# First adaLN vectors by feature with the weights stationary, products taken k-tile by k-tile, rotary angles computed after the first norm, opening reordered

## The chip, the cores and the metric

The kernel runs on one core of a Trainium2 chip. The metric is the device time of one execution in microseconds (us); the figure for the kernel before is the median of 3 runs.

## The reference, cut to what matters

Two layers of a decoder trunk: x is 512 tokens by 1024 features in float32. Each layer forms six vectors of 1024 from the conditioning vector c (adaLN), normalises x, scales and shifts it by two of them, and multiplies by a large weight; q and k are rotated by angles that come from the positions.

```python
c_act = jax.nn.silu(c)
ada = jnp.einsum('bd,de->be', c_act, w_ada[l]) + b_ada[l]
sh_m, sc_m, g_m, sh_f, sc_f, g_f = jnp.split(ada, N_ADA, axis=-1)
h = rmsnorm(x, norm_mix_g[l]) * (1.0 + sc_m) + sh_m
proj = jnp.einsum('bsd,de->bse', h, w_in[l])
ang = positions.astype(jnp.float32)[..., None] * inv_freq
cos, sin = jnp.cos(ang), jnp.sin(ang)
q, k = apply_rope(q, cos, sin), apply_rope(k, cos, sin)   # t1*cos - t2*sin, t2*cos + t1*sin
```

Behind this follow differential attention, two convolution branches, a gated merge and a squared-ReLU MLP, for both layers, and a last rmsnorm. The change touches only the first adaLN vectors, the first norm's scaling, the angles and the order of the opening.

## The kernel before, in words

Activations are kept feature by token: xT[k] holds features 128k to 128k+127 of all 512 tokens, one tile per k-tile, 8 in all. Products run on TensorE in three passes, because each factor is split into a high part that TensorE's fast float32 form holds and a low part: high x high, low x high, high x low (line 145). So a weight chunk needs a cast on ScalarE (the high part, line 394, in the opening line 1270) and a subtraction on VectorE (the low part, line 402, in the opening line 1276), and a product of a 1024-deep k runs 8 x 3 matmuls of 512 columns.

**The opening** is everything up to the first four products (q and k of the first head pair). Its order is written out by hand in the table START (line 38): each word is a unit of work, a letter and a number, and the units are issued from left to right; every engine then works through its own share strictly in that order. SyncE issues the loads: positions (line 1102), x in 8 pieces (line 1110), then four times a quarter of the scale and shift columns of w_ada (8 pieces of 256 KB, line 1118) and of the first two w_in weights (line 1128). The units that matter here:

- y: the sum of squares of a piece of x (ScalarE, line 1225); x and v: four transposes on TensorE (line 1214) and a copy to xT by ScalarE (1217) or VectorE (1219); n and b: the reciprocal root and its broadcast rb.
- e and d: a part of a quarter's scale (e) and shift (d) on VectorE, the last ON_DVE k-tiles of the sum over d (lines 1183 and 1186); r and s: the rest on TensorE as rows, with the activated c broadcast over 128 stationary columns and 256 columns of w_ada moving (line 1193), and a last product that adds VectorE's part (1196); c: ScalarE copies the rows out (1299); t: four transposes turn the rows into columns (1203); q: bias added and gains formed (lines 268 and 272).
- m: two k-tiles of the norm's result are scaled, shifted and split (VectorE 484, ScalarE 487, VectorE 491).
- h and l: high and low part of a quarter of a weight; l14 and l15 also issue the next two weight loads (line 367), which reuse the two staging buffers and so wait for the last reads of those. h16 and l16 are the two parts of the first weight behind the opening.
- p: a quarter (two k-tiles) of one of the four first products; a0 to a7: the angles (VectorE 1148 to 1163, then sine and cosine on ScalarE, 1165 and 1166).

**Behind the opening** the order comes from tasks that are due after so many matmuls. Each of the four products goes through rope: ScalarE copies it out of PSUM (line 712), four loads on SyncE's queue swap its halves (714), VectorE multiplies by cos (717) and sin (719) and adds (720), the result is split (723 to 734) and moved once more by SyncE's queue (738, 739). The first scores of attention (lines 789 and 790) need that. Between the opening and these scores TensorE works on the value products, with one tiny product for the lambdas among them (line 251). SyncE's queue also carries the third weight load (line 367), behind the first eight half-swaps.

Of the kernel before, what the change touches and what calls it, by code (L numbers as in the profile page):

```python
# [10 lines left out]
F32 = mybir.dt.float32  # L11
F32R = mybir.dt.float32r
I32 = mybir.dt.int32
AF = mybir.ActivationFunctionType
ALU = mybir.AluOpType
AX = mybir.AxisListType

P = 128
D = 1024
S = 512  # L20
# [12 lines left out]
WDELAY = 1  # L33
LAM = 2

ON_DVE = ((2, 3), (1, 5), (8, 3), (3, 7))
START = (
# [4 lines left out]
)  # L42
QSTEP, COMB, AWAIT, PWAIT, PERIOD = 2, 2, 3, 4, 9
CPACE, ADA0, ADA1, APACE = 0.71, 2.36, 2.19, 1.62
# [23 lines left out]
SH_M, SC_M, G_M, SH_F, SC_F, G_F = range(6)  # L68
# [3 lines left out]
def kernel(  # L72
# [7 lines left out]
    nc = tc.nc  # L80
    V, A, T, G = nc.vector, nc.scalar, nc.tensor, nc.gpsimd
# [13 lines left out]
    def nm(s):  # L95
        cnt[0] += 1
        return f"{s}{cnt[0]}"
# [3 lines left out]
    def slot(tag, dt=F32, shape=None):  # L101
        return slots.tile(shape or [P, S], dt, tag=tag, name=nm(tag), bufs=SLOTS[tag])

    def ftile(dt=F32, shape=None):
        return slot("f", dt, shape)
# [7 lines left out]
    def ps_t():  # L113
        return psum.tile([P, S], F32, tag="t", name=nm("t"), bufs=3)
# [36 lines left out]
    def pacer(p):  # L151
# [9 lines left out]
    ident = const.tile([P, P], F32, name="ident")  # L161
# [5 lines left out]
    ones1 = const.tile([P, 1], F32, name="ones1")  # L167
# [6 lines left out]
        out=mask[:, 384:512], in_=mask[:, 384:512], pattern=[[-1, 128]],  # L174
# [82 lines left out]
    ada = [const.tile([P, 48], F32, name=f"ada{l}") for l in range(L)]  # L257
    gsc = [const.tile([P, 16], F32, name=f"gsc{l}") for l in range(L)]
    cact = const.tile([P, 8], F32, name="cact")
    ada_known = [set() for _ in range(L)]  # L260

    def ada_done(l, q, n, sm):

        v = q // 8
        dst = ada[l][:, q : q + n]
        ada_known[l].update(range(q, q + n))
        assert (l, 1 if v == SC_F else 0) in written and (l, 0) in written
        V.tensor_tensor(dst, sm, prm[l][:, C_BADA + q : C_BADA + q + n], op=ALU.add)
        if v in (SC_M, SC_F):
            f = (0 if v == SC_M else 8) + q % 8  # L270
            g0 = (C_NMIX if v == SC_M else C_NMLP) + q % 8
            V.scalar_tensor_tensor(out=gsc[l][:, f : f + n], in0=dst, scalar=1.0,
                                   in1=prm[l][:, g0 : g0 + n], op0=ALU.add, op1=ALU.mult)
        if v == G_M:
            V.tensor_scalar(out=dst, in0=dst, scalar1=0.5, scalar2=None, op0=ALU.mult)
# [175 lines left out]
    def bcast(col, n):  # L451

        pt = ps_t()
        for b in range(n):
            T.transpose(pt[:, b * P : (b + 1) * P], col[:, b : b + 1].to_broadcast([P, P]), ident)  # L455
        return pt
# [14 lines left out]


    xT = [xpool.tile([P, S], F32, name=f"xT{k}") for k in range(KD)]

    def modulate(l, f, rb, hh, ks, t0=0, t1=S):

        sv = (SH_M if f == 0 else SH_F) * 8
        assert all(q + k in ada_known[l] for k in ks for q in (sv, sv + 8))
        n = t1 - t0
        u = {}  # L480
        for k in list(ks) + [None]:
            if k is not None:
                u[k] = ftile()
                V.scalar_tensor_tensor(
                    out=u[k][:, :n], in0=xT[k][:, t0:t1], scalar=gsc[l][:, f * 8 + k : f * 8 + k + 1],
                    in1=rb[:, :n], op0=ALU.mult, op1=ALU.mult)
                A.activation(hh[k][0][:, t0:t1], u[k][:, :n], AF.Identity,
                             bias=ada[l][:, sv + k : sv + k + 1])
            if len(u) > (1 if k is not None else 0):
                j = min(u)  # L490
                V.scalar_tensor_tensor(
                    out=hh[j][1][:, t0:t1], in0=u.pop(j)[:, :n], scalar=ada[l][:, sv + j : sv + j + 1],
                    in1=hh[j][0][:, t0:t1].bitcast(F32), op0=ALU.add, op1=ALU.subtract)

    def new_h():
        return [(slot("h", F32R), slot("h", F32R)) for _ in range(KD)]
# [602 lines left out]
    rc = const.tile([P, 2], F32, name="rc")  # L1099
    A.dma_start(rc, rope_c)  # L1100
    posi = slot("at", I32)
    nc.sync.dma_start(posi, positions.to_broadcast([P, S]))
    prm_task = params(0)
    next(prm_task)
    x2 = x.rearrange("b s d -> (b s) d")
    xin = [None] * 8
    for hh in range(2):
        for i in range(NTB):
            t = xin[2 * i + hh] = slot("cv")
# [3 lines left out]
    def fetch(v, qt):  # L1113

        res = []
        for j in range(4):
            r = slot(next(stage), F32, [P, 2, 256])
            nc.sync.dma_start(r, w_ada[0, 256 * j : 256 * j + 256, v * D + qt * 256 : v * D + qt * 256 + 256]
                              .rearrange("(k p) e -> p k e", p=P))
            res.append(r)  # L1120
        return res

    raws += [wraw.tile([P, 8, 256], F32, tag="raw", name=nm("raw")) for _ in range(2)]
    quarters = []
    for qt in range(4):
        quarters.append((fetch(SC_M, qt), fetch(SH_M, qt)))
        for raw, (src, c0, _) in zip(raws, specs):
            nc.sync.dma_start(raw[:, 2 * qt : 2 * qt + 2, :],
                              src[256 * qt : 256 * qt + 256, c0 : c0 + 256].rearrange("(k p) e -> p k e", p=P))

    pt = ps_t()
    T.transpose(pt[:, :8], crow, ident[:8, :8])
# [35 lines left out]
    h = new_h()  # L1168
    parts = [adap.tile([P, 512], F32, tag="araw", name=nm("part")) for _ in range(2)]

    def part(qt, v):
        return parts[qt % 2][:, v * 256 : v * 256 + 256]

    def partial(qt, vs):

        for k in range(8):
            for v in vs:
                k0 = 8 - ON_DVE[qt][v]
                if k < k0:
                    continue  # L1180
                r = quarters[qt][v][k // 2][:, k % 2, :]
                if k == k0:
                    V.tensor_scalar(out=part(qt, v), in0=r, scalar1=cact[:, k : k + 1],
                                    scalar2=None, op0=ALU.mult)
                else:
                    V.scalar_tensor_tensor(out=part(qt, v), in0=r, scalar=cact[:, k : k + 1],
                                           in1=part(qt, v), op0=ALU.mult, op1=ALU.add)

    def rows_of(qt, v, pt):

        n = 8 - ON_DVE[qt][v]
        for k in range(n):
            T.matmul(pt[:, v * 256 : v * 256 + 256], cact[:, k : k + 1].to_broadcast([P, P]),  # L1193
                     quarters[qt][v][k // 2][:, k % 2, :], start=k == 0, stop=k == 7)
        if n < 8:
            T.matmul(pt[:, v * 256 : v * 256 + 256], ones1.to_broadcast([P, P]), part(qt, v),
                     start=n == 0, stop=True)

    def turn(row):

        pt = ps_t()
        for a in range(4):
            T.transpose(pt[:, a * P : a * P + P], row[:, a * P : a * P + P], ident)
        return pt

    def quarter_done(qt, pt):
        pv = pt.rearrange("p (a b) -> p a b", a=4)
        ada_done(0, SC_M * 8 + 2 * qt, 2, pv[:, 0:2, 0])
        ada_done(0, SH_M * 8 + 2 * qt, 2, pv[:, 2:4, 0])

    def x_turned(k, eng):
        pt = ps_t()
# [23 lines left out]
        V.tensor_scalar(out=ms, in0=ms, scalar1=1.0 / D, scalar2=None, op0=ALU.mult)  # L1236
        box["y0"] = rstd(ms, 4)

    w1, qk, q_rows, q_cols, w_tasks = [], [], {}, {}, []
    first = {}  # L1240
    box = {}
    ang_task, lam_task = angles(), lambdas()
# [47 lines left out]
            spawn(rope(first[i], qk, i))  # L1290
            run_due()

    def rows_scale(qt):
        q_rows[qt] = ps_t()
        rows_of(qt, 0, q_rows[qt])

    def rows_copy(qt):
        row = ftile()
        A.copy(row, q_rows[qt])
        q_rows[qt] = row  # L1300

    units = dict(
        x=lambda k: x_turned(k, A),
        v=lambda k: x_turned(k, V),
        y=square, n=lambda _: rms(), w=warm,
        i=lambda _: next(prm_task),
        z=lambda _: next(lam_task),
        a=lambda _: next(ang_task, None),
        b=lambda _: box.update(rb=bcast(box["y0"], 4)),
        e=lambda qt: partial(qt, (0,)),  # L1310
        d=lambda qt: partial(qt, (1,)),
        f=lambda qt: partial(qt, (0, 1)),
        r=rows_scale,
        s=lambda qt: rows_of(qt, 1, q_rows[qt]),
        c=rows_copy,
        t=lambda qt: q_cols.update({qt: turn(q_rows[qt])}),
        q=lambda qt: quarter_done(qt, q_cols[qt]),
        m=lambda qt: modulate(0, 0, box["rb"], h, (2 * qt, 2 * qt + 1)),
        h=high, l=low,
        p=lambda n: first_product(n // 4, n % 4),  # L1320
    )
# [7 lines left out]
    for l in range(L):  # L1329
        merged = mixer(l, h, qk, NF if l else 4)  # L1330
        f = []
        h = closing(l, G_M, merged, l, 1,
                    lambda pp, i: relu2(pp, f, ff_tags(0, i)))
        if l + 1 < L:
            pace["ada"] = APACE
        f = mlp(l, h, f, NF)
        if l + 1 < L:
            qk = []
            h = closing(l, G_F, f, l + 1, 0, lambda pp, i: rope(pp, qk, i))
# [38 lines left out]
```

## Time and profile before

| | |
|---|---|
| median of 3 runs | 1906.89 us (1906.71 to 1907.18) |
| profiled execution, whole time | 1904.28 us |
| its span, first to last instruction | 1902.5 us |
| TensorE matmuls busy | 1874.3 us (99% of the span) |
| VectorE, ScalarE busy | 1256.0 us (66%), 785.8 us (41%) |
| mean granted TensorE clock | 0.997 |

The profile shows one execution. An engine's row in a timeline gives its start and duration, how many instructions of one kind it merges, and in brackets the idle time before it with the instruction that ended the wait. The chain of waits follows the work that ended last back through whatever released each step. PE is TensorE, PEld its weight loads, DVE VectorE, ACT ScalarE, SP SyncE; a q behind a name means its queue of issued instructions. A float32 product that is not in the fast form shows as two records of MATMUL.

### The profile page before, as it was taken

The numbers are of one execution on the slowest core, as the hardware profiler recorded it, in microseconds if no ns is written. First come the engines' busy times: TensorE is split into PE (matmuls) and PEld (weight loads), VectorE is DVE, ScalarE is ACT, GpSimd is POOL, SyncE is SP. The second block draws the span as 40 slices with busy tenths as digits, with TensorE's granted clock in tenths as the row PEclk, the third lists the DMA queues.
The fourth block names the chain that finished last, engine by engine and source line by source line (L and its number), as shares of the span: only waits on it lengthen the run. The fifth ranks groups of instructions, "written<-read, shape, count | busy, mean of one in ns | idle before, by whom it ended". The sixth has DMA issues, their size and how long they took to land.

```text
span 1902.5 us, 24972 instructions
## 1 busy us (share of the span) xinstructions
PE 1874.3 (99%) x9565; PEld 1599.9 (84%) x9565; DVE 1256.0 (66%) x2139; ACT 785.8 (41%) x1420; POOL 63.4 (3%) x109
## 2 busy tenths in 40 slices
PE   8999999999999999999999999999999999999998
PEld 6788888888889888888898888888888898888888
DVE  7788789996676556565677777898654563333336
ACT  4466652223333524333445666322243353424253
POOL 1011010000000000000000000000000000000000
PEclk9999999999999999999999999999999999999999
DMA  8644323444554455555535442232233422223221
GB/s 272 181 130 126 101 67 98 151 138 145 166 178 135 139 178 195 177 185 182 171 97 142 123 122 73 89 104 96 67 100 100 133 89 89 89 93 106 89 89 67
DMA packets 211527, 241.20 MB, mean 127 GB/s; under 512 B 10408, under 2 KB 178480, under 8 KB 211408
## 3 DMA queue, kind: packets, MB, share of 16 engines
q1 hardware_dynamic: 210480, 239.38, 40.6%
q8 instruction: 75, 1.23, 0.3%
q0 software_dynamic: 768, 0.23, 0.1%
q14 instruction: 44, 0.36, 0.1%
q10 hardware_dynamic: 160, 0.01, 0.0%
HBM read 216.50 MB, written 2.10 MB: 115 GB/s over the span
## 4 chain that ended last, share of the span: by engine, by line
PE 93%; DMA 3%; DVE 2%; issue 1%; SPq 1%; ACT 1%; POOL 0%; POOLq 0%; DVEq 0%; ACTq 0%
PE mm L145 83%; PE s L145 3%; DMA f<-f 2%; PE t L817 1%; PE s L789 1%; PE s L790 1%; PE t L806 1%; SPq L714 1%; PE t L1193 1%; PE t L455 0%; PE t L303 0%; PE t L825 0%; POOL st L438 0%; DVE f L719 0%; PE t L1214 0%
## 5 line engine op out<-in xcount | busy, mean ns | idle before, releaser
L145 PE MATMUL mm<-h,wh 128*128 128x512 f32 x2720 | 851.3, 392 | 0.0
L145 PEld LDWEIGHTS mm<-h,wh 128*128 128x128 f32 x2720 | 509.6, 188 | 103.3
L145 PE MATMUL mm<-h,wl 128*128 128x512 f32 x1360 | 533.6, 392 | 0.0
L394 ACT CAST wh<-raw 128x1024 fp32r<-128x1024 f32 (+1 forms) x308 | 308.9, 1005 | 407.2 <-PE mm L145 358.2
L402 DVE TENSOR_TENSOR wl<-raw,wh 128x1024 fp32r<-128x1024 f32 (+1 forms) x308 | 358.2, 1166 | 69.6 <-ACT wh L394 65.9
L145 PE MATMUL mm<-qk,wh 128*128 128x512 f32 (+1 forms) x1024 | 300.2, 376 | 0.0
L145 PEld LDWEIGHTS mm<-h,wl 128*128 128x128 f32 x1360 | 256.2, 188 | 51.9
L145 PEld LDWEIGHTS mm<-qk,wh 128*128 128x128 f32 x1024 | 188.2, 188 | 35.1
L145 PE MATMUL mm<-qk,wl 128*128 128x512 f32 (+1 forms) x512 | 192.6, 376 | 0.0
L912 DVE SCALAR_TENSOR_TENSOR cv<-v,caw,cv 128x511 f32<-128x511 f32 (+14 forms) x240 | 176.0, 733 | 4.2
L499 DVE SCALAR_TENSOR_TENSOR xT<-mm,ada,xT 128x512 f32<-128x512 f32 (+1 forms) x81 | 56.0, 691 | 151.2 <-PE mm L145 151.0
L281 DVE SCALAR_TENSOR_TENSOR araw<-araw,cact,araw 128x512 f32<-128x512 f32 x140 | 104.6, 747 | 25.2 <-DMA araw<-in_w_ada_dram 24.7
L145 PEld LDWEIGHTS mm<-qk,wl 128*128 128x128 f32 x512 | 96.3, 188 | 17.2
L1059 ACT ACTIVATE f<-mm 128x512 f32<-128x512 f32 x60 | 35.9, 598 | 160.6 <-PE mm L145 160.6
L145 PE MATMUL mm<-o,wh 128*128 128x512 f32 (+1 forms) x320 | 95.5, 381 | 0.0
L145 PE MATMUL mm<-v,wh 128*128 128x512 f32 (+1 forms) x320 | 94.9, 379 | 0.0
L145 PE MATMUL mm<-wh,h 128*128 128x256 f32 x448 | 84.1, 284 | 0.0
L761 ACT ACTIVATE cv<-cv,st 128x128 f32<-128x128 f32 (+3 forms) x128 | 71.0, 558 | 25.6 <-DVE st L754 25.2
L1033 DVE SCALAR_TENSOR_TENSOR f<-f,mm 128x512 f32<-128x512 f32 x38 | 26.1, 687 | 83.6 <-PE mm L145 83.6
L469 DVE TENSOR_TENSOR qk<-f,qk 128x512 fp32r<-128x512 f32 x38 | 26.3, 691 | 77.4 <-ACT qk L466 77.2
L438 POOL TENSOR_TENSOR st<-st,nhalf 128x4 f32<-128x4 f32 (+2 forms) x29 | 31.2, 1076 | 1368.0 <-DVE st L460 1013.4
L145 PEld LDWEIGHTS mm<-wh,h 128*128 128x128 f32 x448 | 70.8, 191 | 0.4
(259 smaller groups left out, 2282.9 us busy)
## 6 DMA issues: line engine op xcount, KB each, us to landing
raw<-in_w_in_dram SPq DMA_DIRECT2D x66, 1024.0 KB, 5.2
raw<-in_w_ff_dram SPq DMA_DIRECT2D x64, 1024.0 KB, 5.4
araw<-in_w_ada_dram SPq DMA_DIRECT2D x160, 256.0 KB, 3.0
f<-f SPq DMA_DIRECT2D x128, 64.0 KB, 2.0
qk<-qk SPq DMA_DIRECT2D x64, 128.0 KB, 2.6
raw<-in_w_c_out_dram SPq DMA_DIRECT2D x8, 1024.0 KB, 5.0
raw<-in_w_out_dram SPq DMA_DIRECT2D x8, 1024.0 KB, 5.0
qk<-in_w_ada_dram SPq DMA_DIRECT2D x16, 256.0 KB, 6.0
```

Source lines behind the costliest of these rows:

```text
L145: T.matmul(ps, lhsT, rhs, start=start, stop=stop)
L281: V.scalar_tensor_tensor(out=part, in0=r, scalar=cact[:, k : k + 1], in1=part, op0=ALU.mult, op1=ALU.add)
L394: A.copy(h_, r_)
L402: V.tensor_tensor(l_, r_, h_.bitcast(F32), op=ALU.subtract)
L438: G.tensor_tensor(y, v[:, :n], nhalf[:, :n], op=ALU.pow)
L469: V.tensor_tensor(lo, src, hi.bitcast(F32), op=ALU.subtract)
L499: V.scalar_tensor_tensor(out=xT[e][:, t0:t1], in0=pp[:, t0:t1], scalar=g[:, e : e + 1], in1=xT[e][:, t0:t1], op0=ALU.mult, op1=ALU.add)
L714: nc.sync.dma_start(sw[32 * q : 32 * q + 32, :], t[32 * (q ^ 1) : 32 * (q ^ 1) + 32, :])
L761: A.activation(p[cc][:, :n], p[cc][:, :n], AF.Exp, bias=nb[:, cc : cc + 1], scale=-1.0, accum_out=l0[:, i : i + 1] if cc == 0 else s1)
L912: V.scalar_tensor_tensor(out=ac[:, s:], in0=glu[j][:, : S - s], scalar=wk, in1=ac[:, s:], op0=ALU.mult, op1=ALU.add)
L1033: V.scalar_tensor_tensor(out=t, in0=t, scalar=1.0, in1=pp, op0=ALU.add, op1=ALU.mult)
L1059: A.activation(r, pp, AF.Relu)
```

## The change

The scale and shift columns are no longer made as rows and turned. In the new units r and s the 128 x 128 block of w_ada is the stationary operand and the one column of c moves, so the result stands by feature at once; units c and t (row copy, four transposes) are gone. ON_DVE is a little larger (34 k-tiles on VectorE, before 32). The unit m is split into u (scale, and the high part) and g (the low part), one k-tile at a time, and e and d are issued by single k-tiles. The load of positions is issued behind all loads of the opening, and the angles a0 to a7 stand behind the first norm, nearly at the end of START. Eleven products of the identity with itself (w11) stand ahead of the first transposes. Five of the x tiles are copied by VectorE, before four.

```diff
-ON_DVE = ((2, 3), (1, 5), (8, 3), (3, 7))
+ON_DVE = ((5, 4), (1, 4), (5, 4), (7, 4))
-    "i0 a0 y1 x1 a1 a2 y0 i1 y2 a3 v0 a4 x2 v7 y3 a5 v5 e0 y4 y7 y6 y5 v3 n h2 d0 r0 h0 l2 z "
...
+    "l8 p5 d37 l14 h10 l15 g4 g5 r31 l10 i2 s30 l11 s31 p8 q3 l9 h12 u6 u7 l13 l12 g6 h16 g7 a0 a1 "
+    "a2 a3 p11 p10 p9 l16 a4 a5 a6 a7 p12 p13 p14 p15"
...
-    nc.sync.dma_start(posi, positions.to_broadcast([P, S]))
...
+    nc.sync.dma_start(posi, positions.to_broadcast([P, S]))
...
-            T.matmul(pt[:, v * 256 : v * 256 + 256], cact[:, k : k + 1].to_broadcast([P, P]),
-                     quarters[qt][v][k // 2][:, k % 2, :], start=k == 0, stop=k == 7)
-        if n < 8:
-            T.matmul(pt[:, v * 256 : v * 256 + 256], ones1.to_broadcast([P, P]), part(qt, v),
-                     start=n == 0, stop=True)
...
+            T.matmul(dst, quarters[qt][v][k // 2][:, k % 2, b * P : b * P + P], cact[:, k : k + 1],
+                     start=k == 0, stop=k == 7)
+        if n < 8:
+            T.matmul(dst, part(qt, v)[:, b * P : b * P + P], ones1, start=n == 0, stop=True)
...
+    def scaled(k):
+        u_[k] = ftile()
+        V.scalar_tensor_tensor(out=u_[k], in0=xT[k], scalar=gsc[0][:, k : k + 1], in1=box["rb"],
+                               op0=ALU.mult, op1=ALU.mult)
+        A.activation(h[k][0], u_[k], AF.Identity, bias=ada[0][:, SH_M * 8 + k : SH_M * 8 + k + 1])
+
+    def scaled_low(k):
+        V.scalar_tensor_tensor(out=h[k][1], in0=u_.pop(k), scalar=ada[0][:, SH_M * 8 + k : SH_M * 8 + k + 1],
+                               in1=h[k][0].bitcast(F32), op0=ALU.add, op1=ALU.subtract)
```

How the instructions move. The end of the opening on VectorE before: h are the low parts of the normed input, wl the last low part of the opening's weights, f_624 the copy of the first product, cv_632 the high part of the first weight behind the opening.

```order
L484 SCALAR_TENSOR_TENSOR f_607<-xT_111,gsc_101,t_367 128x512
L491 SCALAR_TENSOR_TENSOR h_237<-f_604,ada_99,h_236 128x512
L491 SCALAR_TENSOR_TENSOR h_239<-f_607,ada_99,h_238 128x512
L1276 TENSOR_TENSOR wl_246<-raw_143,wh_245 128x256
L717 TENSOR_TENSOR f_640<-f_624,cos_t 128x512
L402 TENSOR_TENSOR cv_653<-raw_584,cv_632 128x512
```

The same place on VectorE now, from the last h on; at_120 are the positions, at_222 and at_223 the angles, rc the frequencies, cv_638 and cv_639 the low part of the first weight behind the opening.

```order
L1275 SCALAR_TENSOR_TENSOR h_239<-f_603,ada_99,h_238 128x512
L1130 CAST at_222<-at_120 128x512
L1131 TENSOR_SCALAR at_222<-at_222,rc 128x512
L1133 TENSOR_SCALAR at_223<-at_222 128x512
L1135 TENSOR_SCALAR at_223<-at_223 128x512
L1138 SCALAR_TENSOR_TENSOR at_222<-at_223,at_222 128x512 x2
L404 TENSOR_TENSOR cv_638<-raw_559,cv_609 128x512
L404 TENSOR_TENSOR cv_639<-raw_559,cv_610 128x512
L1138 SCALAR_TENSOR_TENSOR at_222<-at_223,at_222 128x512
L1140 TENSOR_SCALAR at_223<-at_222 128x512
L1142 SCALAR_TENSOR_TENSOR at_223<-at_222,at_223 128x512
L1145 TENSOR_SCALAR at_222<-at_222 128x512
```

All eleven angle instructions (one more L1145 follows) now stand between the last h and the first multiplication by cos, and the two low parts of the next weight stand among them.

ScalarE before, from the last two h to the first rope copies; h_236 and h_238 are high parts of the normed input, f_624 and f_646 copies of the first two products, cv_632, cv_633 and wh_638 high parts of weights. (Sine and cosine stand 18 instructions earlier, behind the cast of wh_247.)

```order
L487 ACTIVATE h_236<-f_604,ada_99 128x512
L487 ACTIVATE h_238<-f_607,ada_99 128x512
L712 COPY f_624<-mm_444 128x512
L394 CAST cv_632<-raw_584 128x512
L394 CAST cv_633<-raw_584 128x512
L394 CAST wh_638<-raw_584 128x1024
L712 COPY f_646<-s_456 128x512
```

ScalarE now, the same place; f_655 is the copy of the first product.

```order
L1272 ACTIVATE h_236<-f_600,ada_99 128x512
L1272 ACTIVATE h_238<-f_603,ada_99 128x512
L396 CAST cv_609<-raw_559 128x512
L396 CAST cv_610<-raw_559 128x512
L1147 ACT_TABLE_LOAD
L1147 ACTIVATE sin_t<-at_222,rc 128x512
L1148 ACTIVATE cos_t<-at_223 128x512
L694 COPY f_655<-mm_451 128x512
L396 CAST wh_664<-raw_559 128x1024
L694 COPY f_672<-s_476 128x512
```

Ahead of the copy of the first product now stand the two casts of the next weight, a table load, the sine and the cosine. From the rows that follow these on, all five engines issue the same instructions in the same order as before.

More of the change, by code (lines that the diff above doesn't have):

```diff
@@ L473 @@
     xT = [xpool.tile([P, S], F32, name=f"xT{k}") for k in range(KD)]
[L475 to L493, printed above, removed]
     def new_h():
@@ L1172, in part @@
         return parts[qt % 2][:, v * 256 : v * 256 + 256]
[L1174 to L1187, printed above, removed]
@@ L1189, in rows_of, with partial @@
-    def rows_of(qt, v, pt):
+    def partial(qt, k, v):
+        k0 = 8 - ON_DVE[qt][v]
+        if k < k0:
+            return
+        r = quarters[qt][v][k // 2][:, k % 2, :]
+        if k == k0:
+            V.tensor_scalar(out=part(qt, v), in0=r, scalar1=cact[:, k : k + 1],
+                            scalar2=None, op0=ALU.mult)
+        else:
+            V.scalar_tensor_tensor(out=part(qt, v), in0=r, scalar=cact[:, k : k + 1],
+                                   in1=part(qt, v), op0=ALU.mult, op1=ALU.add)
@@ L1191, in rows_of, with columns @@
+    def columns(qt, v, b):
+        if v == 0 and b == 0:
+            q_cols[qt] = ps_t()
         n = 8 - ON_DVE[qt][v]
+        dst = q_cols[qt][:, 2 * v + b : 2 * v + b + 1]
         for k in range(n):
-            T.matmul(pt[:, v * 256 : v * 256 + 256], cact[:, k : k + 1].to_broadcast([P, P]),
-                     quarters[qt][v][k // 2][:, k % 2, :], start=k == 0, stop=k == 7)
+            T.matmul(dst, quarters[qt][v][k // 2][:, k % 2, b * P : b * P + P], cact[:, k : k + 1],
+                     start=k == 0, stop=k == 7)
@@ L1195, in rows_of @@
         if n < 8:
-            T.matmul(pt[:, v * 256 : v * 256 + 256], ones1.to_broadcast([P, P]), part(qt, v),
-                     start=n == 0, stop=True)
[L1199 to L1204, printed above, removed]
+            T.matmul(dst, part(qt, v)[:, b * P : b * P + P], ones1, start=n == 0, stop=True)
     def quarter_done(qt, pt):
-        pv = pt.rearrange("p (a b) -> p a b", a=4)
-        ada_done(0, SC_M * 8 + 2 * qt, 2, pv[:, 0:2, 0])
-        ada_done(0, SH_M * 8 + 2 * qt, 2, pv[:, 2:4, 0])
+        ada_done(0, SC_M * 8 + 2 * qt, 2, pt[:, 0:2])
@@ L1211, in x_turned @@
+        ada_done(0, SH_M * 8 + 2 * qt, 2, pt[:, 2:4])
     def x_turned(k, eng):
@@ L1237, in rms @@
         box["y0"] = rstd(ms, 4)
-    w1, qk, q_rows, q_cols, w_tasks = [], [], {}, {}, []
+    w1, qk, u_, q_cols, w_tasks = [], [], {}, {}, []
     first = {}
@@ L1291, in first_product @@
             run_due()
[L1293 to L1300, printed above, removed]
+    def scaled(k):
[6 more added lines that the diff above has]
+                               in1=h[k][0].bitcast(F32), op0=ALU.add, op1=ALU.subtract)
     units = dict(
@@ L1309 @@
         b=lambda _: box.update(rb=bcast(box["y0"], 4)),
[L1310 to L1316, printed above, removed]
+        e=lambda n: partial(n // 10, n % 10, 0),
+        d=lambda n: partial(n // 10, n % 10, 1),
+        r=lambda n: columns(n // 10, 0, n % 10),
+        s=lambda n: columns(n // 10, 1, n % 10),
         q=lambda qt: quarter_done(qt, q_cols[qt]),
-        m=lambda qt: modulate(0, 0, box["rb"], h, (2 * qt, 2 * qt + 1)),
+        u=scaled, g=scaled_low,
         h=high, l=low,
```

7 rows, old and new, of the table START are left out of this document.

## The prediction

> **What bounds the kernel now.** The first line of the page gives the span; the profiled execution took 1904.28 us as a whole, 1.8 more, and the median of the runs is 1906.89, 2.6 above that. I work out a difference on the profiled execution and add it to the median.
>
> ```profile
> span 1902.5 us, 24972 instructions
> ```
>
> TensorE is busy nearly throughout, and the order of instructions shows no difference on any engine behind the opening. So the change is worth what it does to the moment at which the unchanged rest starts. I read next what TensorE waits for in the first 140 us (waiter, releaser: us in total, times, longest), and the stretches around these waits (stretch, PE, PEld, DVE, ACT, POOL busy, clock, DMA).
>
> ```profile
> PE t L207 <- DMA f<-in_norm_mix_g_dram: 6.1, 1, 6.1
> PE s L789 <- DMA qk<-f: 3.2, 1, 3.2
> PE s L789 <- DVE st L754: 1.8, 2, 1.1
> ```
> ```profile
> 10.90:51.83 40.93, 40.79 (x195) 34.57 (x195) 36.79 (x88) 21.32 (x48) 6.84 (x12) 1.00 0.85 269
> 75.00:80.00 5.00, 3.77 (x11) 3.11 (x12) 2.12 (x7) 0.99 (x4) 0.00 (x0) 0.66 0.79 200
> ```
>
> In the opening TensorE never stops (40.79 of 40.93 us) and VectorE is close behind (36.79). The first wait for something else is 3.2 us, in front of the first attention scores (L789), and the clock drops behind it. What sets the time of these scores is read from the chain of waits (start, us, what) and from SyncE's queue.
>
> ```profile
> 8.96 5.40 PE t L1214 x24
> ...
> 31.98 0.44 PE t L1203 x4
> ...
> 53.87 0.59 ACT f L712
> ...
> 59.87 5.71 DMA raw<-in_w_in_dram
> ...
> 65.61 1.06 ACT wh L394
> ...
> 76.65 0.45 PE s L789
> ...
> 77.31 4.97 PE mm L145 x16
> ...
> 82.76 3.65 PE mm L145 x16
> ```
> ```profile
> 48.27 4.35 SPq L367 DMA_DIRECT2D raw<-in_w_in_dram  x2
> 54.48 5.29 SPq L714 DMA_DIRECT2D f<-f  x8
> ```
>
> ScalarE copies the first product at 53.87. Then SyncE's queue issues the eight half-swaps of the first two products without a pause (54.48, for 5.29 us), and only then the third weight load (its transfer from 59.87). ScalarE, which works in order, needs that load for a cast at 65.61, ahead of the copy of the fourth product, and the rest of rope follows to the scores at 76.65. Every step waits for the one before: from the copy at 53.87 to the scores is a fixed distance, and TensorE, out of other work 3.2 us earlier, waits for its end.
>
> **The change part by part.** *Columns on TensorE.* A record of the old form (256 columns moving) takes 0.216 us, from the first to the next group below (17.61 to 19.77 for 10); the new form (128 x 128 stationary, one column) stands in the trace as line 447.
>
> ```profile
> 17.61 2.32 PE L1193 MATMUL t<-qk,cact 128*128 128x256 f32 x10
> 19.77 0.59 PE L1196 MATMUL t<-part,ones 128*128 128x256 f32 x2
> ...
> 454.83 0.95 PE L447 MATMUL t<-inv,f 128*128 128x1 f32 x8
> 455.63 0.64 PE L303 MATMUL t<-ident,araw 128*128 128x128 f32 x4
> ```
> ```profile
> L447 PEld LDWEIGHTS t<-inv,f 128*128 128x128 f32 x16 | 2.1, 191 | 0.2
> ```
>
> Before: 32 products and 8 closings, two records each, 80 x 0.216 = 17.3 us, and 16 turns at 0.11 (0.44 for 4), 1.8: 19.1 us. Now 30 products in two halves and 16 closings, 76, two records each: 152 x 0.10 = 15.2 us (455.63 - 454.83 over 8). The other end, weight loads of 191 ns one after the other, would give 29.0. I take 0.10, the spacing seen, so TensorE has 3.9 us less. The 11 warming products stand in the first wait of 6.1 us and cost nothing there; if they bring the clock up, the first 24 transposes cost 0.11 instead of 0.225 each (5.40 for 24), 2.8 us less.
>
> *VectorE.* If TensorE does less, VectorE is the next late engine of the opening.
>
> ```profile
> 10.90 0.69 DVE L1219 COPY xT<-t 128x512 f32<-128x512 f32 x1 [1.09 <-PE t L1214]
> 11.51 0.68 DVE L1156 SCALAR_TENSOR_TENSOR at<-at,at 128x512 f32<-128x512 f32 x1
> ...
> 13.29 0.42 DVE L1158 TENSOR_SCALAR at<-at 128x512 f32<-128x512 f32 x1
> 13.75 0.69 DVE L1160 SCALAR_TENSOR_TENSOR at<-at,at 128x512 f32<-128x512 f32 x1
> ...
> 18.81 0.76 DVE L1163 TENSOR_SCALAR at<-at 128x512 f32<-128x512 f32 x2
> ...
> 50.41 1.42 DVE L491 SCALAR_TENSOR_TENSOR h<-f,ada,h 128x512 fp32r<-128x512 f32 x2
> 51.74 0.42 DVE L1276 TENSOR_TENSOR wl<-raw,wh 128x256 fp32r<-128x256 f32 x1
> ```
> ```profile
> L1186 DVE SCALAR_TENSOR_TENSOR part<-o,cact,part 128x256 f32<-128x256 f32 x9 | 4.4, 485 | 0.8 <-DMA o<-in_w_ada_dram 0.5
> ```
>
> Of the 36.79 us in 10.90 to 51.83 the angles take 0.68 + 0.42 + 0.69 + 0.76 = 2.55 and leave. A fifth xT copy (0.69) and two more partial sums (2 x 0.485 = 0.97) come: 36.79 - 2.55 + 0.69 + 0.97 = 35.9 us of work, and with the idle time of now (40.93 - 36.79 = 4.1) 40.0 in all. It starts at 10.90 as now, or at 10.0: the first tile turned is now VectorE's own, so four cold transposes, 0.9 us, fewer stand ahead of it. (That x is issued before the positions now could add some tenths.) So the last h stands at 50.0 to 50.9; as the second end can only come nearer, I take 50.2, against 51.83 for today's end.
>
> *Angles and the first weight behind the opening.* This is the price.
>
> ```profile
> 5.40 0.43 DVE L1148 CAST at<-at 128x512 f32<-128x512 int32 x1 [1.78 <-DMA at<-in_positions_dram]
> 6.46 0.49 DVE L1149 TENSOR_SCALAR at<-at,rc 128x512 f32<-128x512 f32 x1 [0.63 <-DMA rc<-rope_c_dram]
> 6.98 0.43 DVE L1151 TENSOR_SCALAR at<-at 128x512 f32<-128x512 f32 x1
> ...
> 55.09 1.29 DVE L402 TENSOR_TENSOR cv<-raw,cv 128x512 fp32r<-128x512 f32 x2
> ```
> ```profile
> 28.40 0.72 ACT L1165 ACTIVATE sin_t<-at,rc 128x512 f32<-128x512 f32 x1
> 29.03 0.61 ACT L1166 ACTIVATE cos_t<-at 128x512 f32<-128x512 f32 x1
> ...
> 54.35 1.14 ACT L394 CAST cv<-raw 128x512 fp32r<-128x512 f32 x2
> ```
> ```profile
> DMA to landing us min/median/max: 5.2/5.7/6.7
> ```
>
> On VectorE the angles up to the two L1138 take 0.43 + 0.49 + 0.43 + 0.43 + 2 x 0.68 = 3.1, to 53.3. Next in its row stand the low parts of the next weight, which need that weight. Its load waits for the last reads of the staging buffers; they stand two h (1.42) and a low part (0.42) ahead of 50.2, at 48.4, so it is issued as today (48.27) and lands after 5.7, at 54.1 (bounds 5.2 and 6.7, the last row above, of the three loads of line 367 there). From the landing: a cast 0.57, two low parts 1.29, the last L1138 0.69, 0.42, 0.69, the clamps 0.76, sine 0.72, cosine 0.61: 5.75 one after the other, 5.3 with sine beside the second clamp and issue overlapped; I take 5.6. The copy of the first product stands behind the cosine on ScalarE: 54.1 + 5.6 = 59.7. If the load did not hold VectorE, it would be 53.3 + 1.29 + 0.69 + 0.42 + 0.69 + 0.76 + 0.72 + 0.61 = 58.5 (the lower bound, with the last h at 50.2). So the copy moves from 53.87 to 59.7, **5.8 us later**.
>
> What queues behind: the half-swaps, the third weight load and with it the whole fixed distance, 76.65 to 82.4. TensorE is there before that. Its wait at L251, the lambda product, hangs on VectorE's row of rope and moves along:
>
> ```profile
> 64.77 0.35 PE L251 MATMUL t<-st,f 1*128 1x2 f32 x2 [0.76 <-DVE st L246]
> ```
>
> It starts at 70.6 and not 64.77, and as TensorE comes there some 2 us earlier than today's 64.0, it waits about 8. From there to the end of its work were some 8 us (64.77 to 73); a cold start adds half of 3.4, so it is through at about 80.5, ahead of the scores by 2 us or less. The gain on TensorE in the opening (3.9 + 2.8) therefore goes into longer waits. The row copies taken from ScalarE were hidden too (it was busy 21.32 of 40.93).
>
> *Clock.* Behind the 3.2 us wait the granted clock fell (0.66 in 75 to 80), and 16 matmuls took 4.97 us, 3.65 later: 1.3 us, and some 0.2 on the scores. Behind the waits of 1.8 us in all further on it did not fall:
>
> ```profile
> 100.00:110.00 10.00, 8.93 (x67) 8.13 (x66) 9.52 (x22) 7.42 (x17) 0.53 (x1) 1.00 0.73 202
> ```
>
> With 2 us or less I expect it to stay up: **1.5 us gained**; bounds 0, if it falls all the same, and 1.9. The Trainium skill, TensorE: Matmul & The Clock Gate, "Part 1: The HAM clock gate", says that the clock halves after an idle window of about 3.4 us that runs free of the kernel; the trace's drop behind 3.2 us agrees roughly, and by that rule a wait of 2 us keeps the clock: the sum stays as it is, while with a drop it would be 5.8.
>
> Sum: 5.8 - 1.5 = +4.3 us: 1908.6 for the profiled execution, 1911.2 for the median. The waits of 1.8 at later scores could give back some of the 1.5, no more.
>
> **The rivals.** A measurement of this kernel can tell about 0.2%, 3.8 us, from no change. My forecast is over that if the copy stands later than 53.87 + 3.8 + 1.5 = 59.2.
>
> *Not slower: VectorE's front comes earlier* (0.30). Idle time on VectorE halves (4.1 to 2.1) because TensorE delivers columns sooner, so the last h stands at 48.2; the load goes out at 46.4 and lands after 5.2, at 51.6; then VectorE alone decides: the copy at 58.5 - 2.0 = 56.5, or by the load 57.2. That is +3.3 - 1.5 = +1.8, 1908.7. For it: TensorE's 6.7 us; against it: the last quarter's weights land no earlier than its load, and 35.9 us of work fill the time.
>
> *Faster: the scores are held by TensorE, not by rope* (0.06). If the chain has slack I do not see, the 3.9 + 2.8 us count in full: 1900.2. Against it: the rows from 53.87 to 76.65 touch.
>
> *Slower still: two loads at once* (0.12). Today the two loads behind the opening go out 4 us apart (48.27, for 4.35 with the wait); now both buffers come free within 0.4 us. If they share the engines, the first lands with the second: 1 MB, about 3 us at the 350 GB/s below, later. +7.3, 1914.2.
>
> ```profile
> 50.00:51.00 1.00, 1.00 (x6) 0.83 (x5) 0.87 (x2) 1.00 (x2) 0.00 (x0) 1.00 1.01 346
> ```
>
> The Trainium skill, DMA: Bandwidth & Descriptors, "Queues, rings and completion order", says that each DMA engine takes the descriptors of one ring in order; by that the first load is not held by the second and this rival falls. No row here shows two such loads 0.4 us apart.
>
> *TensorE is the bound after all* (0.04): records of 0.19 us would make the columns 29.0 us, 10 more than before, and the copy later by 7 at least: +5.5 or more, 1912.4.
>
> **How the numbers follow.** The forecast has 0.48 (copy at 58.5 to 61 and the clock's 1.5: +3.1 to +5.6). Slower by over 0.2%: most of it, 0.44, and the two slow rivals, 0.16: 0.60. Within 0.2%: the rest, and the first rival: 0.34. Faster: 0.06. The range goes from the first rival's 1908.7, less 0.4 for the clock's other bound and 1.0 if a quarter of the idle time is left, 1907.3, to the two loads' 1914.2; it leaves out the faster case and the ends of the others.
>
> **What would show it.** Right: VectorE's last h at 50.0 to 50.9; the first weight behind the opening lands about 54; the copy of the first product stands behind the cosine at about 59.7; TensorE waits some 8 us at the lambda product and 2 us or less at the first scores, with the clock back at 1.00 there. Wrong: a copy before 59.2 makes it no difference; a wait at the scores that doesn't follow the copy makes the chain wrong; and clock lost twice makes it 1.5 us more.

## The result and the profile after

The kernel after takes 1918.3 us (median of 4 runs, 1915.51 to 1919.99); the kernel before, run beside it, 1907.04 (4 runs). The ratio is put at 1.0064, 95% interval 1.005 to 1.0077 (the two medians alone give 1.0059): slower, above the 1911.2 that I forecast and above the range, which ended at 1914.2. The profiled executions stand 11.2 us apart (1915.51 and 1904.28). One run of e2 below took 2340.15 us, at a mean granted clock of 0.749 in place of 0.99, and is not counted.

```profile
span 1913.7 us, 25128 instructions
```

First the stretches of the opening (stretch, length, PE, PEld, DVE, ACT and POOL busy, granted clock, DMA share, GB/s), of the kernel before:

```profile
15.00:35.00 20.00, 19.86 (x100) 16.81 (x99) 17.14 (x46) 9.69 (x20) 5.35 (x10) 1.00 1.10 348
35.00:55.00 20.00, 20.00 (x94) 16.46 (x93) 16.93 (x39) 8.66 (x18) 1.50 (x3) 1.00 0.54 168
```

and of the kernel after:

```profile
15.00:35.00 20.00, 19.98 (x94) 19.41 (x94) 12.56 (x35) 6.00 (x14) 4.70 (x8) 0.53 1.10 348
35.00:55.00 20.00, 20.00 (x102) 17.38 (x100) 14.48 (x34) 4.73 (x11) 0.00 (x0) 0.79 0.29 94
```

TensorE is as busy as before, and yet its clock is 0.53, then 0.79, in place of 1.00. VectorE's busy time falls from 17.14 to 12.56: it waits. TensorE's timeline in the kernel after shows the price of the columns:

```profile
25.03 3.12 PE L1177 MATMUL t<-cact,qk 128*128 128x1 f32 x14
28.02 0.56 PE L1180 MATMUL t<-ones,part 128*128 128x1 f32 x2
...
33.71 0.63 PE L147 MATMUL mm<-h,wl 128*128 128x512 f32 x1
...
37.06 0.39 PE L147 MATMUL s<-h,wl 128*128 128x512 f32 x1
...
41.71 1.03 PE L1177 MATMUL t<-cact,o 128*128 128x1 f32 x8
42.60 0.36 PE L1180 MATMUL t<-ones,part 128*128 128x1 f32 x2
```

Fourteen column records take 28.02 - 25.03 = 2.99 us, 0.213 each; later, with the clock up (1.00 in 41.71 to 42.60), eight take 42.60 - 41.71 = 0.89, 0.111 each. The dense product behind the columns pays too: at 33.71 a matmul of 512 columns shows 0.63 us, at 37.06 it shows 0.39. VectorE in the same execution:

```profile
32.89 0.16 DVE L270 TENSOR_TENSOR ada<-t,prm 128x2 f32<-128x2 f32 x1 [4.99 <-PE t L1180]
...
55.95 0.16 DVE L270 TENSOR_TENSOR ada<-t,prm 128x2 f32<-128x2 f32 x1 [5.72 <-PE t L1180]
...
58.61 1.41 DVE L1275 SCALAR_TENSOR_TENSOR h<-f,ada,h 128x512 fp32r<-128x512 f32 x2
```

It waits 4.99 and 5.72 us for columns, and the last h ends at 58.61 + 1.41 = 60.02, where I had 50.2. From there the chain of waits of the kernel after:

```profile
58.43 5.16 DMA raw<-in_w_in_dram
63.66 0.63 ACT cv L396
...
69.14 0.48 ACT f L694
...
75.89 5.75 DMA raw<-in_w_in_dram
...
82.62 0.58 ACT f L694
...
93.04 0.30 PE s L771
...
93.46 5.32 PE mm L147 x16
```

It has the links that the prediction names: load, casts, low parts, angles, sine and cosine, copy of the first product (at 69.05 in ScalarE's own row, 15.2 later than before), third load, copy of the fourth, scores (76.65 before, 93.04 now: +16.4). Behind the scores 16 matmuls take 5.32 us: the clock has dropped again (0.71 in 95 to 100). The two longest waits of TensorE up to 140 us:

```profile
PE s L771 <- issue: 3.0, 1, 3.0
PE t L253 <- DVE st L248: 2.9, 1, 2.9
```

Of the 16.4 us only 11.2 are left at the end. Part comes back within 45 us, where before has 1.75 us of TensorE idle in 100 to 120 (18.25 busy of 20.00) and after 0.50 in 116 to 136; most of the rest comes back in the second layer. Its waits before (waiter, releaser: total, times, longest), 1010 to 1130 us, and TensorE's rows at the first of them:

```profile
PE s L789 <- DVE st L754: 3.8, 3, 2.2
```

```profile
1028.02 0.39 PE L789 MATMUL s<-qk,qk 128*128 128x256 f32 x1 [2.16 <-DVE st L754]
...
1029.71 0.63 PE L145 MATMUL mm<-h,wl 128*128 128x512 f32 x1
...
1031.85 0.41 PE L806 MATMUL t<-ident,cv 128*128 128x128 f32 x1
```

The same in the kernel after, 1025 to 1141 us:

```profile
PE s L771 <- DVE st L736: 1.9, 2, 1.7
```

```profile
1042.65 0.39 PE L771 MATMUL s<-qk,qk 128*128 128x256 f32 x1 [1.66 <-DVE st L736]
...
1043.91 0.39 PE L147 MATMUL mm<-h,wl 128*128 128x512 f32 x1
...
1045.05 0.60 PE L788 MATMUL t<-ident,cv 128*128 128x128 f32 x4
```

The kernel before loses the clock behind a wait of 2.16 us (0.63 for a matmul); the kernel after waits 1.66 there and keeps it (0.39). From 1042.65 - 1028.02 = 14.6 the distance shrinks to 1045.05 - 1031.85 = 13.2 within four microseconds. These are instructions that the change does not touch; e3, e5, e7, e8 and e11 below lost the clock about this place too; e1, e2, e4, e6, e9 and e10 did not. The length of the wait goes with it: in these 13 executions the five that waited 2.9 us or more at this place (e8 2.9, e7 3.0, e5 3.2, e3 3.6, e11 4.3) lost the clock, and the five that waited 1.9 or less (after, e1, e4, e9, e10) kept it. In between, 2.2 lost it (before) and 2.4 and 2.6 kept it (e2, e6); what decides there stays open.

### The profile page after: what moved, and what is told of

Its sections match the earlier page's. It is cut to its first block, busy times and chain, and to the rows that moved or that the text cites. A ratio compares the mean times of both kernels' runs of the same rounds, so it can differ in the third digit from the quotient of the medians.

```text
span 1913.7 us, 25128 instructions
## 1 busy us (share of the span) xinstructions
PE 1888.7 (99%) x9643; PEld 1614.8 (84%) x9643; DVE 1256.7 (66%) x2142; ACT 783.2 (41%) x1415; POOL 63.5 (3%) x109
## 4 chain that ended last, share of the span: by engine, by line
PE 94%; DMA 2%; DVE 1%; issue 1%; SPq 1%; ACT 0%; POOL 0%; POOLq 0%; DVEq 0%; ACTq 0%
PE mm L147 83%; PE s L147 3%; PE t L799 2%; PE s L771 1%; PE t L1177 1%; PE s L772 1%; PE t L788 1%; SPq L696 1%; DMA f<-f 1%; PE t L457 1%; DMA raw<-in_w_in_dram 1%; PE t L305 0%; PE t L807 0%; POOL st L440 0%; DMA qk<-in_w_ada_dram 0%
```

## The experiments

The theory after the result: (A) products that move one column let the clock fall, and everything on TensorE runs at half speed until dense products have brought it back; (B) the angles and the next weight ahead of the first rope copy are a price of their own, as predicted. The rival (C): the clock falls because TensorE waits for data in the reordered opening. In e1 to e4 the kernel before took 1907.7 us (19 runs), in e5 to e8 1907.21 (23), in e9 to e11 1906.65 (21); ratios are to these groups (the quotients of the medians lie up to 0.0013 off them).

**e1: the same columns, 128 wide.**

```diff
-        dst = q_cols[qt][:, 2 * v + b : 2 * v + b + 1]
+        dst = q_cols[qt][:, (2 * v + b) * P : (2 * v + b) * P + 128]
...
-            T.matmul(dst, quarters[qt][v][k // 2][:, k % 2, b * P : b * P + P], cact[:, k : k + 1],
+            T.matmul(dst, quarters[qt][v][k // 2][:, k % 2, b * P : b * P + P], cact[:, k : k + 1].to_broadcast([P, 128]),
...
-            T.matmul(dst, part(qt, v)[:, b * P : b * P + P], ones1, start=n == 0, stop=True)
+            T.matmul(dst, part(qt, v)[:, b * P : b * P + P], ones1.to_broadcast([P, 128]), start=n == 0, stop=True)
...
```

> The kernel after, but each column product moves 128 copies of the one column in place of one (the result is 128 equal columns, of which one is read). Theory A (products that move one column let the granted clock fall, and they and the products behind them then run at half speed): the clock stays near 1.00 up to the end of the opening, a column record takes about 0.11 us in place of 0.213, the last h stands at 50 to 53 in place of 60.02, the copy of the first product at 59 to 62 in place of 69.05, and the median is 1908 to 1913. Rival C (the clock falls because TensorE waits for data in the opening, whatever the columns look like): the clock is 0.50 in the same stretches, and the median is 1916 to 1920.

Measured: 1909.96 us (10 runs), ratio 1.0013 (1.0004 to 1.0022), 8.3 below the kernel after (9.0, if each is taken against the kernel before in its own group), with the instructions in the same order. The first stretch, then TensorE's, VectorE's and ScalarE's timelines:

```profile
15.00:35.00 20.00, 18.71 (x136) 17.08 (x135) 16.44 (x43) 7.03 (x17) 4.75 (x8) 1.00 1.10 348
```

```profile
21.92 1.73 PE L1177 MATMUL t<-cact,qk 128*128 128x128 f32 x14
23.48 0.39 PE L1180 MATMUL t<-ones,part 128*128 128x128 f32 x2
...
60.87 0.38 PE L147 MATMUL mm<-wh,h 128*128 128x256 f32 x1 [2.93 <-ACT wh L396]
62.63 0.58 PE L147 MATMUL mm<-wl,h 128*128 128x256 f32 x1 [1.39 <-DVE wl L404]
...
70.19 0.35 PE L253 MATMUL t<-st,f 1*128 1x2 f32 x2 [1.85 <-DVE st L248]
...
83.07 0.44 PE L771 MATMUL s<-qk,qk 128*128 128x128 f32 x1 [4.74 <-DMA qk<-f]
```

```profile
48.73 1.41 DVE L1276 SCALAR_TENSOR_TENSOR h<-f,ada,h 128x512 fp32r<-128x512 f32 x2
```

```profile
53.92 1.14 ACT L396 CAST cv<-raw 128x512 fp32r<-128x512 f32 x2 [5.02 <-DMA raw<-in_w_in_dram]
...
59.30 0.56 ACT L694 COPY f<-mm 128x512 f32<-128x512 f32 x1
```

The clock is 1.00 and fourteen records take 23.48 - 21.92 = 1.56, 0.111 each. The waits of the opening are still there (18.71 busy of 20.00, fewer than after's 19.98), so C falls for this stretch: in the same order, with these waits, the width of the products decides the clock. The last h ends at 50.14, the weight is there at 53.9, the copy stands at 59.30.

**e2: narrow columns, angles early.** The load of positions goes first, the angle units stand among the first transposes.

```diff
-    "w11 z v0 y2 y1 v1 v7 v3 y5 y3 x5 y0 e03 ...
+    "w11 z a0 v0 a1 y2 y1 v1 a2 v7 a3 v3 a4 y5 y3 x5 a5 y0 e03 ... b a6 u1 ... s11 a7 l7 q1 ...
-    ... h16 g7 a0 a1 a2 a3 p11 p10 p9 l16 a4 a5 a6 a7 p12 p13 p14 p15"
+    ... h16 g7 p11 p10 p9 l16 p12 p13 p14 p15"
```

> The kernel after, with the load of positions first in SyncE's queue and the angles a0 to a7 early in the opening; columns as in after. Theory B (the angles between the last h and the first rope copy are a price of their own): from the last h to the copy of the first product 2 to 3 us in place of 9.03, so about 6.5 less, of which VectorE's extra work in the opening takes back 0 to 3: median 1911.5 to 1915. The clock falls in the columns as in after (theory A). If the angles were hidden by the weight load that lands at the same time, the median stays at 1917 to 1919.

Measured: 1914.98 us (median of 3 runs), ratio 1.0051 (1.0031 to 1.0072); only 3.3 below the kernel after, and the intervals of the two ratios overlap. VectorE and ScalarE:

```profile
58.35 0.16 DVE L270 TENSOR_TENSOR ada<-t,prm 128x2 f32<-128x2 f32 x1 [4.71 <-PE t L1180]
...
61.01 1.41 DVE L1275 SCALAR_TENSOR_TENSOR h<-f,ada,h 128x512 fp32r<-128x512 f32 x2
```

```profile
66.20 1.14 ACT L396 CAST cv<-raw 128x512 fp32r<-128x512 f32 x2 [5.02 <-DMA raw<-in_w_in_dram]
67.25 0.58 ACT L694 COPY f<-mm 128x512 f32<-128x512 f32 x1
```

The last h comes 2.4 us later (62.42) and the copy 4.83 behind it in place of 9.03, not the 2 to 3 that I expected: ScalarE's casts for the next weight stand ahead of the copy and now hold it alone. The clock falls as in after (0.56 in 15 to 35).

**e3: both edits.**

> Both edits, 128 moving columns and early angles. If A and B are two separate prices that add: clock near 1.00 in the opening, last h at 51 to 54, copy of the first product 2 to 3 us behind it, the first scores at 75 to 79, the median 1901 to 1908. If what is left over is a third price of the new order, the median stays above 1910.

Measured: 1904.98 us (10 runs), ratio 0.999 (0.998 to 1.0001), 5.0 below e1. ScalarE:

```profile
54.62 1.14 ACT L396 CAST cv<-raw 128x512 fp32r<-128x512 f32 x2 [4.89 <-DMA raw<-in_w_in_dram]
55.67 0.58 ACT L694 COPY f<-mm 128x512 f32<-128x512 f32 x1
```

From the kernel after, the width gives 8.3 and then the angles 5.0. In the other order it is 3.3 for the angles (e2) and then 10.0 for the width; from the few runs of after and e2, whether the two simply add is not shown. With the clock up, B has about the size I gave the step (5.8), though the copy itself comes only 3.6 earlier (59.30 to 55.67). In the profiled execution the clock is at 0.55 in 10 to 17 us, where TensorE waits for x among the transposes, ahead of any column: narrow products are not the only thing that takes it down.

**e4: the kernel before, with the column form alone.** Order and angles as they were; the copies to rows and the turns go.

```diff
...
-        r=rows_scale,
-        s=lambda qt: rows_of(qt, 1, q_rows[qt]),
-        c=rows_copy,
-        t=lambda qt: q_cols.update({qt: turn(q_rows[qt])}),
+        r=lambda qt: [columns(qt, 0, b) for b in range(2)],
+        s=lambda qt: [columns(qt, 1, b) for b in range(2)],
...
```

> The kernel before, order and angles as they were, with only the form of the products changed: blocks of w_ada stationary and one column moving, no row copies and no turns (160 records in place of 80 and 16 turns). Theory A: the clock falls to 0.50 in stretches of the opening, records take 0.21 there, and the opening ends 5 to 15 us later: median 1911 to 1921. Rival (the form is harmless by itself, 160 x 0.11 = 17.6 us in place of 19.1): clock 1.00, median 1904 to 1907.5.

Measured: 1915.51 us (4 runs), ratio 1.0052 (1.0032 to 1.0071). The first stretch:

```profile
15.00:35.00 20.00, 19.43 (x88) 18.92 (x89) 13.71 (x35) 8.44 (x18) 6.76 (x12) 0.51 1.10 347
```

The clock falls in the old order too (0.51): the form does it, not the reordering.

**e8: as e4, 128 wide.**

> As e4 (the kernel before with the column form, no row copies, no turns), but moving 128 equal columns. Theory A: clock 1.00 in the opening, 160 records at 0.11 = 17.6 us in place of 19.1 with the turns, so no loss: median 1904 to 1908.5. If the form costs something beside the clock (more records, other waits on VectorE's sums): 1910 to 1915.

Measured: 1905.07 us (10 runs), ratio 0.9991 (0.9982 to 1.0). Stretch:

```profile
15.00:35.00 20.00, 17.92 (x133) 16.53 (x132) 16.84 (x46) 8.73 (x18) 6.81 (x12) 1.00 1.10 347
```

Between e4 and e8 only the width of the moving operand, and with it of the result, differs: 10.4 us (9.9, each against its own group). The column form as such is harmless or a little better than rows and turns.

**e6, e7, e11: 16, 64 and 96 moving columns** in the kernel after.

> The kernel after with 16 moving columns in the column products. Theory A in its plain form (the clock follows the share of time in which columns move, a record taking 0.11 us at full clock, so 16 of about 128 columns is an eighth): the clock falls to 0.50 in stretches of the opening as with one column, span 1911 to 1915. If any width over one is enough: clock 1.00 to 55, span 1906 to 1909.

> The kernel after with 64 moving columns. Theory A in its plain form: a half share of moving columns, near the border; the clock at 1.00 in most stretches of the opening, span 1906 to 1910. If the clock needs TensorE's array full: 0.50 in some stretches, span 1910 to 1915.

> The kernel after with 96 moving columns. One column, 16 and 64 lost the clock, 128 kept it. If the clock needs about all of the time with columns moving: 0.50 in some stretches between 17 and 35, span 1911 to 1915. If three quarters are enough: 1.00 up to 55, span 1906 to 1909.

Measured: 1916.92, 1916.38 and 1910.52 us, one run each. The first stretch of the one with 16:

```profile
15.00:35.00 20.00, 19.41 (x93) 18.45 (x93) 13.81 (x37) 5.44 (x13) 4.68 (x8) 0.58 1.10 348
```

with 64:

```profile
15.00:35.00 20.00, 19.43 (x97) 18.55 (x96) 13.64 (x38) 6.04 (x14) 4.68 (x8) 0.60 1.10 348
35.00:55.00 20.00, 20.00 (x119) 17.62 (x118) 16.44 (x41) 6.11 (x13) 0.00 (x0) 0.98 0.28 91
```

with 96:

```profile
15.00:35.00 20.00, 18.62 (x136) 17.05 (x136) 16.59 (x43) 7.24 (x17) 4.75 (x8) 1.00 1.10 348
```

A record of 256 columns took 0.216 us, so by estimate 64 columns move for about 0.054 and 96 for 0.081 of the 0.111 that a record takes at full clock: about half of the time, and about three quarters. Here half was not enough, against what I expected of 64, and three quarters were; 64 brought the clock back sooner behind 35 us (0.98, after 0.79). That the share of time counts, and not the number of columns in each product, is not shown.

**e5: e3 with the next weight behind the first copy**, as in the kernel before.

```diff
-    ... g6 h16 g7 p11 p10 p9 l16 p12 p13 p14 p15"
+    ... g6 g7 p11 p10 p9 p12 h16 p13 l16 p14 p15"
```

> As e3 (128 moving columns, early angles), with the high and low part of the first weight behind the opening put back behind the first product's copy, as in the kernel before. If that weight's load (it lands at 54.6 in e3) is what holds the first copy there (55.67, while the product itself is through at 49.5), the copy stands at 50 to 52, the first half-swaps go out 4 to 5 us sooner, the third weight load 1 to 3 us sooner, the first scores at 74.5 to 77 and the median is 1 to 3 us below e3's 1904.98: 1902 to 1904.5. If the chain to the scores hangs on the second copy, which stays behind that weight, the median is e3's within 1 us.

Measured: 1905.13 us (12 runs), ratio 0.9988 (0.9978 to 0.9999): e3's time, and not the 1 to 3 us less that I expected. ScalarE:

```profile
53.93 0.59 ACT L694 COPY f<-mm 128x512 f32<-128x512 f32 x1 [4.04 <-PE mm L147]
...
66.82 1.05 ACT L396 CAST wh<-raw 128x1024 fp32r<-128x1024 f32 x1 [5.73 <-DMA raw<-in_w_in_dram]
67.77 0.58 ACT L694 COPY f<-mm 128x512 f32<-128x512 f32 x1
```

The copy now waits for the product itself; that this was through at 49.5 in e3 was my misreading. Further on the third weight load holds the fourth copy as before. Where e3, e5 and e8 gain their 2 to 3 us on the kernel before, hardly clear of noise, is not shown: in the profiled executions the first scores of e3 and e5 start at 78.33 and 77.49, later than the 76.10 before.

**e9 and e10: the fourth copy ahead of the cast of the third load**, in e5 and in the kernel before.

```diff
-            release(w1[i])
+            if i < 2:
+                release(w1[i])
             spawn(rope(first[i], qk, i))
             run_due()
+            if i == 3:
+                release(w1[2])
+                release(w1[3])
```

> As e5, with the copy of the fourth first product put ahead of the cast that waits for the third weight load (the next two weights are released behind the fourth product). If that load is what now sets the first scores (in e5 the load lands, cast 66.82, copy of the fourth product 67.77, scores at about 77 with a TensorE wait of 5.3), the copy stands at 61 to 62, the second eight half-swaps take 5 to 6 us in place of 10.17, the scores stand at 72 to 74, TensorE waits 2 us or less there and the median is 3 to 5 us below e5's 1905.13: 1900 to 1902. If the wait only moves on (to the third weight itself, or to the queue of moves), the median is e5's within 1 us.

> The same single edit on the kernel before. If the third weight load sets the first scores there too (cast 65.61, copy 66.56, scores 76.65, wait 3.2), 2 to 3 us less and the clock kept behind the scores, 1.5 more: median 1902.5 to 1905. If the wait only moves on: 1906 to 1908.

Measured: e9 1902.97 us (11 runs), ratio 0.998 (0.9972 to 0.9989); e10 1906.75 (11 runs), ratio 1.0006 (0.9997 to 1.0015). TensorE in e9:

```profile
76.42 0.30 PE L771 MATMUL s<-qk,qk 128*128 128x128 f32 x1 [3.12 <-issue]
```

The scores are not at 72 to 74: the wait only moves on (rival), in e10 with no gain at all. e9 is nevertheless 0.2% faster than the kernel before, and 2.2 us below e5, where the rival allowed 1. In its profile the clock stays at 1.00 from 10 us on, behind a wait of 3.12 us too; whether that is what the 2.2 us come from isn't shown, and its other runs have mean clocks of 0.995 to 0.998, the kernel before 0.995 to 0.999.

## Why the prediction was wrong

- **Columns on TensorE: this step failed.** "I take 0.10, the spacing seen" came from eight records between dense products, at full clock. The record itself was nearly right (0.111 at full clock, e1), but tens of them in a row take the clock down, each then costs 0.213, and the dense products behind them run at half speed as well. For the clock of the opening the sum had no term at all; its one clock term stands behind the scores. I had 15.2 us for the columns. From the first column record of each stretch to the next other product they take 6.5 + 11.0 + 4.5 + 0.4 + 2.6 = 25.0 us in the kernel after, and, less waits, about 18 in e1. I had TensorE 6.7 us ahead of today; it was late, with VectorE waiting 4.99 and 5.72 us for it. Of the 6.7, the 2.8 us on the transposes did not come either: the first column record starts at 14.33, the first row product before at 14.15; the transposes now wait 1.0 us for the loads of x and 1.0 for VectorE's copy. The rival "TensorE is the bound after all", to which I gave 0.04, had 29.0 us for the columns, by weight loads of 191 ns. Its size was nearer, its cause was not the right one, and it left out the neighbours. The miss is 7.1 us (1918.3 - 1911.2), the width alone is worth 8.3 here and 10.4 in the old order.
- The Trainium skill, TensorE: Matmul & The Clock Gate, "Part 1: The HAM clock gate", says that the clock follows how busy TensorE has lately been. The profile's busy share is not that measure here: it shows 19.98 us busy of 20.00 with the clock at 0.53.
- **VectorE the next late engine, last h at 50.2:** wrong in the kernel after (60.02), right in e1 (50.14), where a column record costs nearly what I had assumed. The figure is in part luck: in e1 VectorE starts at 8.29 and not 10.0, and idles 5.8 us (36.05 busy of 41.85) and not 4.1.
- **Angles and weight behind the opening:** right. From the landing (58.43 + 5.16 = 63.59) to the copy at 69.05 it is 5.5 us, predicted 5.6; in e1 the weight is there at 53.9 (54.1) and the copy stands at 59.30 (59.7). Two loads issued 0.5 us apart did not slow the first (5.16 us; I had 5.7): that rival falls. e3 against e1 prices the placement of the angles at 5.0.
- **Fixed distance from the copy to the scores:** nearly. It was 22.8 us; 24.0 in the kernel after (69.05 to 93.04) and 24.2 in e1 (59.30 to 83.53).
- **The clock's 1.5 us behind the scores: wrong.** TensorE waits 3.0 us there in the kernel after and 4.74 in e1, and the clock falls again. I let the lambda wait take 8 us and a cold start follow. It took 2.9, and in e1 1.85: the lambda product itself stood at 70.19 (I had 70.6), but TensorE had waited before it, 2.93 us for ScalarE's cast of a next weight and 1.39 for its low part, which stand behind the late copy too and which I left out. The clock fell there (0.71 in 60 to 65) and was back at the lambda product, so TensorE was through at 78.3 and not 80.5, and the scores came 1.1 later than the 82.4 of the prediction (83.53 is the row of e1 that answers to 76.65).
- **What comes back further on:** I allowed at most the 1.5 us. In the profiled executions 5.2 of the 16.4 us came back, so the time does not simply follow the first scores.
- **As a whole:** with the clock held up in the opening, the copy comes 5.4 us later, about as the prediction describes (5.8). That e1's 1909.96 lies near the forecast of 1911.2 is partly luck: its first scores come 6.9 later, the 1.5 for the clock was not gained, and yet its median is 2.3 above the kernel before and not 4.3; what gives the rest back is not shown. Against 1907.7 the steps, taken in this order, are -2.7 for e3 (the new order and form without the two prices), +5.0 for the late angles, +8.3 for the one moving column: 10.6 in sum.

## What to carry to other kernels

A busy TensorE need not be a warm one: price a stream of products that move few columns at half clock, and the dense work behind it too, until the granted clock of that stretch says otherwise. Where the width of the moving operand does not set the pace, widening it (here to 96 or 128 columns) cost no time in the products and kept the clock. A spacing read from a short burst among dense products is not the price of a long stream.

## What the runs showed of the hardware beside this

- The pace of column records on a 128 x 128 block did not change with the width, but followed the granted clock: 0.21 us with 1, 16 and 64 columns at 0.50, 0.111 with 1 and with 128 at 1.00. Weight loads were busy throughout (2.99 of 2.99 us in 25.03 to 28.02 of the kernel after), so I take them to set it; no run tests that alone.
- The share of time with columns moving that kept the clock at 1.00 lay between about a half (64 columns) and three quarters (96), from one execution each.
- The clock fell once behind a wait of 2.16 us (before, at 1028 us) and stayed up once behind one of 3.12 (e9, at 76 us), so no single length decides.
